# RWKV-7 recurrence of a two-layer decoder step: when the rows of v, the keys and the bonus product are issued

## The chip, the cores and the metric

The kernel runs on one core of a Trainium2 chip. The metric is the device time of one execution in microseconds; the time shown for a kernel is the median of its runs.

## What is computed

One inference step of two layers over a prompt of 2048 tokens (16 meta tokens ahead of it) and a sample batch of 8 x 4 tokens, width 1024. Layer 0 is sliding-window attention, layer 1 is RWKV-7 time mixing with 16 heads of 64. The change lies in the second one:

```python
def step(S, inp):                      # per token, S is (value, key) per head
    r_t, w_t, k_t, v_t, a_t, b_t = inp
    sa = jnp.einsum('bhvk,bhk->bhv', S, a_t)
    S = S * w_t + sa[..., None] * b_t + v_t[..., None] * k_t
    return S, jnp.einsum('bhvk,bhk->bhv', S, r_t)

y = (y - mean) * lax.rsqrt(var + GN_EPS)       # per head
y = y * ln_g + ln_b
bonus = jnp.sum(r_h * k_h * r_k, axis=-1, keepdims=True) * v_h
y = (y + bonus) * jax.nn.silu(g)
out = jnp.einsum('btw,wd->btd', y, w_out)
```

The final hidden state is normalised and returned, with the new attention window, the state S and the shift row.

## The kernel before, in words

The first two thirds of the program compute attention and the projections of the second layer, and leave their results in DRAM: keys and decay factors (bk), receptance and the like (ar), v, a bonus factor per token and head (bo), gates and first-layer outputs. The last third, from about 1580 us on, is the recurrence. It goes over 17 units of the prompt: a unit of meta tokens, then 16 units of 128 tokens, each of four chunks of 32 tokens. The tokens of a chunk are done at once; the state S goes from chunk to chunk.

*A chunk* is `chain` (line 1422). PE multiplies the state block Z with L into C (C<-Z,L), ACT copies the result to R0s, PE multiplies with TT, the inverse of a triangular matrix per head (C<-R0s,TT), ACT writes that into Z, PE multiplies Z with the transposed keys LS (C<-Z,LS), and DVE scales the result by the decay pe into the Z of the next chunk (Z<-C,pe). There are four Z in turn; their rows of v come by DMA (Z<-v).

*Ahead of time*, for later units: `keys` (1374) transposes BK on PE into kt and ACT copies it to LS; `scores` (948) multiplies L with BK into pz, which ACT copies to LAs and DVE masks back into L; `inverse` (976) sends LAs through DRAM (la_d) to LA, one row per chunk and head, and POOL solves the triangular systems in some sixty small products (XT<-LA,X and X<-X,XT), scales them (X<-X,ln) and sends them through DRAM (tt_d) to TT. The unit two further on (s in the code) gets its scores while unit u runs, and the inversion for the next unit runs on POOL at that time.

*Behind the chain*: `outputs` (1465) gives Y for two chunks at a time. `group_norm` (1583) of a unit runs during the next one, in steps between yields: it fetches the rows of v again (vt), takes the mean, multiplies vt by the bonus (line 1602), subtracts the mean into ytm, and lets ACT square it; DVE sums the squares into var, POOL takes the root (lines 1621 and 1622), and DVE scales ytm by var, lng and lnb and adds vt. `gate` and `project_out` multiply by the gate, transpose, and project with `dense_steps`.

*The order of the work* is written by hand. `steady` (1765), for units 2 to 14, runs per chunk: first product, left-over steps of the last chunk, side work (Y, scores, key transposes of the next unit in chunk 3), a step of the norm, the solve, keys of the unit's own second half in chunk 0, another step of the norm, the state update, loads. `in_order` (1752) then binds DVE, ACT and POOL to the order in which this was written. DMAs of SP are not bound by it: they are placed by a scheduler, behind the last Z load that was written ahead of them (`released`, 1405). A queue works in order: a DMA at its head that waits holds those behind it. Without an engine named, a load goes out on SP; with `s_` on ACT.

In `steady`, BK and the second half of L of the unit two on are loaded on ACT after the chunk's third step in chunk 0 (lines 1832 to 1837), and half 0 of L for the unit three on in chunk 3 (1841), so that it is there when its unit comes to be the second one on. There are four BK tiles, two to a unit, so BK of unit s takes the place of unit u's, once its keys are transposed; six L tiles; two vt tiles; one h tile and one ytm tile.

Of the kernel before, what the change touches and what calls it, by code (L numbers as in the profile page):

```python
# [14 lines left out]
ALU = mybir.AluOpType  # L15
# [15 lines left out]
def tile_hybrid_step(ctx: ExitStack, tc: tile.TileContext, a, o, c):  # L31
# [842 lines left out]
    def all_of(gen):  # L874
        for _ in gen:
            pass
# [391 lines left out]
    with ExitStack() as ph:  # L1268
# [314 lines left out]
        def group_norm(u):  # L1583
# [12 lines left out]
            for x in range(2):  # L1596
                ms_ = mean[:n, x * 8:x * 8 + 8]
                v_.tensor_reduce(out=ms_, in_=u.Y[x][:n], axis=AX.X, op=ALU.add)
                v_.tensor_scalar(out=ms_, in0=ms_, scalar1=1.0 / 64, scalar2=None, op0=ALU.mult)
                if vts and x == 0:  # L1600
                    for e in range(2):
                        tt(v_, vts[e], vts[e], u.bont[:n, 8 - e * 8:16 - e * 8].unsqueeze(2).broadcast_to([n, 8, 64]), ALU.mult)
                    yield MARK
                if x == 0:
                    u.ytm = u.Ys if u.kind == "s" else lt.tile([P, 2, 8, 64], F32, name="ytm", tag="ytm", bufs=1)
                    y = u.ytm[:n].rearrange("p e g d -> p (e g) d")
                for e, ps_ in HS:
                    if u.kind == "s" and e == 0:
                        tt(v_, u.ytm[:n, x], u.Y[x][:n], ms_.unsqueeze(2).broadcast_to([n, 8, 64]), ALU.subtract)
                    elif u.kind != "s":  # L1610
                        tt(v_, u.ytm[64 * x:64 * x + 64, e], u.Y[x][ps_],
                           mean[ps_, x * 8:x * 8 + 8].unsqueeze(2).broadcast_to([64, 8, 64]), ALU.subtract)
                yield MARK if vts and x == 0 else 2.3
# [6 lines left out]
            with tc.high_priority(offset=5000):  # L1620
                g_.tensor_scalar(out=var[:n], in0=var[:n], scalar1=1.0 / 64, scalar2=64e-5, op0=ALU.mult, op1=ALU.add)
                tt(g_, var[:n], var[:n], mhalf[:n], ALU.pow)
            yield MARK
            tt(v_, y, y, bc(var), ALU.mult)
            yield MARK
# [139 lines left out]
        def steady(i, u, pe):  # L1765
# [9 lines left out]
            for ch in range(4):  # L1775
# [36 lines left out]
                run(pe[ch], 1.2)  # L1812
                next(rec)
                with released():
                    if ch == 0 and i > 2:
                        all_of(keys(u, 1))
                    if ch == 3:
                        all_of(kt)
                        inv[s.idx] = inverse(s)
                        next(inv[s.idx])  # L1820
                    else:
                        next(inv.get(i + 1, idle()), None)
                if ch < 3:
                    run(norm, to=MARK)
                else:
                    norms_[u.idx] = group_norm(u)
                    run(norms_[u.idx], to=MARK)
                    run(norms_[u.idx], to=MARK)
                run(pe[ch], 1.9)
                next(rec, None)  # L1830
                with released():
                    if ch == 0:
                        first = L0s.pop(s.idx, None)
                        load_BK(s, s_)
                        s.L.append(first or load_L(s, 0, s_))
                        s.L.append(load_L(s, 1, s_))
                        small_loads(s)
                    if ch == 2 and i + 1 in inv:
                        load_TT(us[i + 1])
                    if ch == 3 and i + 3 < len(us):  # L1840
                        L0s[i + 3] = load_L(us[i + 3], 0, s_)
                run(pe[ch], to=MARK)
                rests.append(pe[ch])
                for part in PLAN.get((i, ch), ()):
                    with released():
# [214 lines left out]
```

## Time and profile before

| | |
|---|---|
| median of 3 runs | 2597.73 us (2594.54 to 2601.28) |
| profiled execution | 2601.98 us, span of its instructions 2600.2 us |
| busy share of the span | PE 86%, PEld (weight loads) 60%, DVE 65%, ACT 45%, POOL 40% |
| mean granted clock of TensorE | 0.937 of full speed |
| moved by DMA | 312.99 MB, 120 GB/s over the span |
| chain that ended last, by engine | PE 50%, DVE 18%, issue 10%, ACT 9%, DMA 8%, POOL 4% |

The shares are averages over stages that differ. The recurrence's steady part, some 1720 to 2420 us, is the stage that the change touches; there a row of the timeline tells when an instruction started, how long it took, how long its engine had been idle before it and what ended that. "issue" as a releaser means that the profile shows nothing that was waited for. SPq and ACTq rows are DMA issues on those queues, not transfers.

### The profile page before, as it was taken

Reading aid. Unit: us, or ns where it says so; the run is one execution under the profiler, and the core shown is the slowest. Engines: PE = TensorE matmul, PEld = TensorE weight load, DVE = VectorE, ACT = ScalarE, POOL = GpSimd, SP = SyncE. Lnnn points to the kernel's source line nnn. Section 1 sums busy time; section 2 is a strip of 40 time slices with the busy share of each in tenths; the row PEclk is TensorE's granted clock in tenths of the full one; section 3 lists DMA queues with packets and bytes.
Section 4 is the critical chain, followed back from the end, with each engine's and each line's share of the span. In section 5 each row is a group of like instructions: output and inputs, shape, how many; then the busy total and the mean of one; then the engine's idle time right before and its main releaser. Section 6 shows DMA issues by size and latency. Waiting matters only on the chain.

```text
span 2600.2 us, 60852 instructions
## 1 busy us (share of the span) xinstructions
PE 2238.5 (86%) x24932; PEld 1547.7 (60%) x24932; DVE 1687.0 (65%) x3181; ACT 1169.5 (45%) x2799; POOL 1044.8 (40%) x1572
## 2 busy tenths in 40 slices
PE   6999999899999898999999997567777777777897
PEld 5877777767845446676666785354444444444553
DVE  7586675567749887665656665645666566666684
ACT  6676455555523335454434444233443434434432
POOL 4242123222112335433333333147566666656613
PEclk9999999999999998999999998778898988889999
DMA  8433122331447664322222216564544545454423
GB/s 202 122 106 117 63 69 94 107 115 62 150 138 226 210 205 153 98 81 96 86 102 85 93 67 192 140 182 118 132 105 114 135 115 131 103 126 124 106 67 76
DMA packets 346235, 312.99 MB, mean 120 GB/s; under 512 B 205546, under 2 KB 282218, under 8 KB 344131
## 3 DMA queue, kind: packets, MB, share of 16 engines
q1 hardware_dynamic: 327219, 278.03, 36.4%
q10 hardware_dynamic: 17120, 27.27, 4.0%
q0 software_dynamic: 1616, 3.79, 0.7%
q8 instruction: 196, 3.21, 0.5%
q14 instruction: 84, 0.69, 0.1%
HBM read 191.15 MB, written 119.84 MB: 120 GB/s over the span
## 4 chain that ended last, share of the span: by engine, by line
PE 50%; DVE 18%; issue 10%; ACT 9%; DMA 8%; POOL 4%; SPq 2%; POOLq 0%; ACTq 0%; DVEq 0%
PE pd L38 29%; PE po L38 5%; PE C L38 5%; DVE xm L47 4%; DMA BK<-bk 2%; DVE xpr L44 2%; ACT ssb L41 2%; PE pz L38 2%; SPq L50 2%; PE Y L38 2%; PE sc L38 1%; PE oT L38 1%; DMA wst<-in_rwkv_w_in 1%; DMA L<-ar 1%; PE kt L1385 1%
## 5 line engine op out<-in xcount | busy, mean ns | idle before, releaser
L38 PEld LDWEIGHTS <-yp 128*128 128x128 f16 x1488 | 141.1, 99 | 165.2 <-issue 12.8
L47 DVE SCALAR_TENSOR_TENSOR xm<-dx,mu,xn 128x256 f32<-128x256 f32 (+2 forms) x432 | 199.8, 523 | 48.9 <-POOL dx L44 47.6
L44 POOL TENSOR_TENSOR X<-X,XT 128x126 f32<-128x126 f32 (+24 forms) x458 | 202.4, 442 | 35.5
L44 POOL TENSOR_TENSOR XT<-LA,X 128x126 f32<-128x126 f32 (+24 forms) x458 | 180.4, 394 | 39.7 <-DVE X L44 6.0
L38 PE MATMUL C<-Z,L 128*32 128x64 f32 x2048 | 49.5, 247 | 170.4 <-issue 159.9
L38 PE MATMUL pd<-xp,wq 128*128 128x256 f16 (+2 forms) x1728 | 186.0, 266 | 11.4 <-DVE qp L47 8.0
L38 PE MATMUL pd<-wg,xg 128*128 128x512 f16 (+1 forms) x816 | 193.1, 384 | 0.7 <-issue 0.7
L38 PE MATMUL po<-wo,yp 128*128 128x512 f16 x768 | 188.9, 389 | 0.0
L38 PE MATMUL pd<-wvv,xpr 128*128 128x512 f16 (+1 forms) x816 | 187.4, 387 | 0.0
L38 PE MATMUL pd<-xpr,w 128*128 128x256 f16 (+2 forms) x1728 | 186.0, 267 | 0.0
L38 PE MATMUL pd<-xp,wg 128*128 128x256 f16 (+2 forms) x1728 | 182.6, 266 | 0.9 <-DVE xp L44 0.5
L38 PE MATMUL pd<-xpr,wkk 128*128 128x256 f16 (+2 forms) x1728 | 179.5, 264 | 0.0
L38 PEld LDWEIGHTS <-wq 128*128 128x128 f16 x1728 | 159.3, 99 | 32.7 <-DVE qp L47 9.2
L44 POOL TENSOR_TENSOR ssb<-ssb,bias 128x512 f32<-128x512 f32 x64 | 86.4, 1355 | 223.9 <-DVE ssb L462 185.5
L38 PEld LDWEIGHTS <-w 128*128 128x128 f16 x1728 | 157.5, 99 | 27.0 <-issue 9.7
L38 PEld LDWEIGHTS <-wg 128*128 128x128 f16 x1728 | 159.2, 99 | 21.5 <-issue 4.0
L38 PEld LDWEIGHTS <-wkk 128*128 128x128 f16 x1728 | 158.2, 98 | 15.6 <-issue 0.4
L38 PE MATMUL pd<-w,yp 128*128 128x512 f16 x720 | 162.9, 384 | 3.3 <-DMA yp<-y 3.3
L44 POOL TENSOR_TENSOR ps<-wst,ps 128x1024 f16<-128x1024 f32 x32 | 69.5, 2171 | 220.0 <-ACT wst L41 201.7
L38 PEld LDWEIGHTS C<-Z,L 128*32 128x32 f32 x2048 | 38.9, 126 | 195.8 <-issue 192.3
L41 ACT ACTIVATE R0s<-C 128x256 f32<-128x256 f32 x65 | 25.0, 385 | 274.9 <-PE C L38 269.9
L38 PEld LDWEIGHTS <-xpr 128*128 128x128 f16 (+1 forms) x816 | 79.1, 100 | 102.6 <-issue 17.5
(357 smaller groups left out, 4913.2 us busy)
## 6 DMA issues: line engine op xcount, KB each, us to landing
wst<-in_rwkv_w_in SPq DMA_DIRECT2D x32, 512.0 KB
wsp<-ps SPq DMA_DIRECT2D x32, 512.0 KB
x<-in_x_prompt SPq DMA_DIRECT2D x29, 512.0 KB
xn<-xn SPq DMA_DIRECT2D x14, 1028.0 KB
ar<-aro SPq DMA_DIRECT2D x28, 512.0 KB
bk<-bko SPq DMA_DIRECT2D x28, 512.0 KB
BK<-bk ACTq DMA_DIRECT2D x26, 512.0 KB
L<-ar ACTq DMA_DIRECT2D x52, 256.0 KB
```

The costliest lines, as they stand in the source:

```text
L38: return t_.matmul(out=out, lhsT=lhsT, rhs=rhs, start=start, stop=stop, **kw).ins
L41: return s_.activation(out=out, in_=in_, func=func, **kw).ins
L44: return e.tensor_tensor(out=out, in0=in0, in1=in1, op=op).ins
L47: v_.scalar_tensor_tensor(out=out, in0=in0, scalar=scalar, in1=in1, op0=op0, op1=op1)
L50: return (eng or nc.sync).dma_start(out=out, in_=in_).ins
L1385: t_.transpose(out=ps[:w * 64, j].rearrange("p e d -> p (e d)"), in_=u.BK[half][:, j, 2 * c2:2 * c2 + w, :].rearrange("p c x -> p (c x)"), ...
```

## The change

It does four things in the recurrence. In `group_norm` the multiplication of vt by the bonus moves from ahead of the subtraction of the mean to behind the variance, into a step of its own, and `steady` runs one step of the norm more at the end of chunk 0. The norm of a unit is begun, and so its vt requested, at the end of chunk 2 instead of in chunk 3. BK and the first half of L for the unit two on are requested on SP, right behind the key transposes of chunk 0 and ahead of the copies to LS; only the second half of L stays on ACT. And the loading of L for the unit three on now stands under `if ch == 3` inside `if ch == 2`, so it is never reached, and every first half of L is loaded in chunk 0's code.

```diff
--- before.py
+++ after.py
@@ -1598,8 +1598,6 @@
                 v_.tensor_reduce(out=ms_, in_=u.Y[x][:n], axis=AX.X, op=ALU.add)
                 v_.tensor_scalar(out=ms_, in0=ms_, scalar1=1.0 / 64, scalar2=None, op0=ALU.mult)
                 if vts and x == 0:
-                    for e in range(2):
-                        tt(v_, vts[e], vts[e], u.bont[:n, 8 - e * 8:16 - e * 8].unsqueeze(2).broadcast_to([n, 8, 64]), ALU.mult)
                     yield MARK
                 if x == 0:
                     u.ytm = u.Ys if u.kind == "s" else lt.tile([P, 2, 8, 64], F32, name="ytm", tag="ytm", bufs=1)
@@ -1620,6 +1618,9 @@
             with tc.high_priority(offset=5000):
                 g_.tensor_scalar(out=var[:n], in0=var[:n], scalar1=1.0 / 64, scalar2=64e-5, op0=ALU.mult, op1=ALU.add)
                 tt(g_, var[:n], var[:n], mhalf[:n], ALU.pow)
+            yield MARK
+            for e, vt in enumerate(vts):
+                tt(v_, vt, vt, u.bont[:n, 8 - e * 8:16 - e * 8].unsqueeze(2).broadcast_to([n, 8, 64]), ALU.mult)
             yield MARK
             tt(v_, y, y, bc(var), ALU.mult)
             yield MARK
@@ -1812,8 +1813,13 @@
                 run(pe[ch], 1.2)
                 next(rec)
                 with released():
-                    if ch == 0 and i > 2:
-                        all_of(keys(u, 1))
+                    if ch == 0:
+                        kt = keys(u, 1) if i > 2 else idle()
+                        next(kt, None)
+                        first = L0s.pop(s.idx, None)
+                        load_BK(s)
+                        s.L.append(first or load_L(s, 0))
+                        all_of(kt)
                     if ch == 3:
                         all_of(kt)
                         inv[s.idx] = inverse(s)
@@ -1823,23 +1829,23 @@
                 if ch < 3:
                     run(norm, to=MARK)
                 else:
-                    norms_[u.idx] = group_norm(u)
-                    run(norms_[u.idx], to=MARK)
                     run(norms_[u.idx], to=MARK)
                 run(pe[ch], 1.9)
                 next(rec, None)
                 with released():
                     if ch == 0:
-                        first = L0s.pop(s.idx, None)
-                        load_BK(s, s_)
-                        s.L.append(first or load_L(s, 0, s_))
                         s.L.append(load_L(s, 1, s_))
                         small_loads(s)
                     if ch == 2 and i + 1 in inv:
                         load_TT(us[i + 1])
+                if ch == 2:
+                    norms_[u.idx] = group_norm(u)
+                    run(norms_[u.idx], to=MARK)
                     if ch == 3 and i + 3 < len(us):
                         L0s[i + 3] = load_L(us[i + 3], 0, s_)
                 run(pe[ch], to=MARK)
+                if ch == 0:
+                    run(norm, to=MARK)
                 rests.append(pe[ch])
                 for part in PLAN.get((i, ch), ()):
                     with released():
```

DVE at the boundary between two units and in the first chunk of the next, before (vt are rows of v, Z_19045 the state that chunk 0 begins with; Y has a number per unit):

```order
L47 SCALAR_TENSOR_TENSOR yp<-yps,yp 128x512
L1598 TENSOR_REDUCE mean<-Y_22365 128x8
L1599 TENSOR_SCALAR mean<-mean 128x8
L44 TENSOR_TENSOR vt<-vt,bont 128x512 x2
L44 TENSOR_TENSOR Z_19045<-C,pe 64x256 x4
L47 SCALAR_TENSOR_TENSOR gt<-gt,pd 128x512
```

and now:

```order
L47 SCALAR_TENSOR_TENSOR yp<-yps,yp 128x512
L1598 TENSOR_REDUCE mean<-Y_22365 128x8
L1599 TENSOR_SCALAR mean<-mean 128x8
L44 TENSOR_TENSOR Z_19045<-C,pe 64x256 x4
L47 SCALAR_TENSOR_TENSOR gt<-gt,pd 128x512
L44 TENSOR_TENSOR gt<-gt,ytm 128x512
```

The multiplication has left the place ahead of Z_19045. It stands now a chunk later, behind Z_19046, the state for chunk 1:

```order
L1616 TENSOR_REDUCE var<-Y_22714 128x8
L44 TENSOR_TENSOR Z_19046<-C,pe 64x256 x4
L47 SCALAR_TENSOR_TENSOR h_22753<-po,h_22753 128x512
L44 TENSOR_TENSOR vt<-vt,bont 128x512 x2
L44 TENSOR_TENSOR ytm<-ytm,var 128x1024
L44 TENSOR_TENSOR L<-pz,smk 64x512 x4
```

SP at the end of a unit, before (la_d, LA, tt_d and TT belong to the inversions, pe and bont are the decay and bonus factors):

```order
L50 DMA la_d<-LAs 32x32x32 x2
L50 DMA pe<-pe_169 128x32
L50 DMA bont<-bo_205 128x16
L50 DMA tt_d<-X 64x16x32 x2
L50 DMA LA<-la_d 64x1024 x2
L50 DMA vt<-v_104 128x512
L50 DMA TT<-tt_d 64x1x512 x2
L50 DMA vt<-v_104 128x512
L50 DMA out_y_prompt<-h_21362 128x1024
L50 DMA h_22060<-h_3_86 128x1024
```

and now:

```order
L50 DMA la_d<-LAs 32x32x32 x2
L50 DMA L<-ar_156 64x1024
L50 DMA tt_d<-X 64x16x32 x2
L50 DMA LA<-la_d 64x1024
L50 DMA vt<-v_104 128x512 x2
L50 DMA LA<-la_d 64x1024
L50 DMA TT<-tt_d 64x1x512 x2
L50 DMA L<-ar_156 64x1024
L50 DMA pe<-pe_169 128x32
L50 DMA bont<-bo_205 128x16
L50 DMA out_y_prompt<-h_21357 128x1024
L50 DMA h_22055<-h_3_86 128x1024
```

Both vt stand between the two LA and ahead of both TT; half of L stands ahead of tt_d and half behind TT; pe and bont have gone behind them.

ACT in chunk 0, behind the squares (Y), before:

```order
L41 ACTIVATE Y_21667<-ytm 128x512
L41 ACTIVATE Y_22021<-ytm 128x512
L50 DMA BK<-bk_147 128x4x256 x2
L50 DMA L<-ar_156 64x1024 x2
L41 ACTIVATE R0s<-C 128x256
L41 ACTIVATE po,ssq_22061<-h_22060 128x512
```

and now:

```order
L41 ACTIVATE Y_21667<-ytm 128x512
L41 ACTIVATE Y_22016<-ytm 128x512
L50 DMA L<-ar_156 64x1024 x2
L41 ACTIVATE R0s<-C 128x256
L41 ACTIVATE po,ssq_22056<-h_22055 128x512
L41 ACTIVATE LAs<-pz 32x2x128 x4
```

The two BK requests are gone from ACT. SP in the same chunk 0 now, from the rows of v for chunks 2 and 3 on:

```order
L50 DMA Z_19044<-v_105 32x512
L50 DMA Z_19047<-v_105 32x512 x2
L50 DMA Z_19044<-v_105 32x512
L50 DMA xg<-xg_128 128x16x128
L50 DMA BK<-bk_147 128x4x256 x2
L50 DMA Z_19046<-v_106 32x512
```

BK has left ACT and stands on SP behind xg, the gate's input; the pair of L requests that ACT made in chunk 3 for the unit three on is gone, and the first half of L is the one that SP has taken over above.

## Rows read from the trace of the kernel before

**Rows 1.** Waits, all engines, 1850 to 2340 us: engine line waited for: us in total, times, longest
```profile
DVE vt L44 <- DMA vt<-v: 90.4, 18, 7.7
POOL LA L44 <- DMA LA<-la_d: 72.8, 10, 7.6
POOL var L1621 <- DVE var L1618: 62.1, 9, 7.7
```

**Rows 2.** Timeline of DVE: start us, us, engine line op tiles, count [idle before <-releaser]
```profile
2180.55 2.07 DVE L44 TENSOR_TENSOR vt<-vt,bont 128x512 f32<-128x512 f32 x1 [1.95 <-DMA vt<-v]
2189.11 0.97 DVE L44 TENSOR_TENSOR vt<-vt,bont 128x512 f32<-128x512 f32 x1 [6.49 <-DMA vt<-v]
2190.00 1.72 DVE L44 TENSOR_TENSOR Z<-C,pe 64x256 f32<-64x256 f32 x4
```

**Rows 3.** Timeline of PE, chunk 0 of a steady unit
```profile
2191.82 1.08 PE L38 MATMUL C<-Z,L 128*32 128x64 f32 x32 [9.02 <-issue]
...
2194.54 1.08 PE L38 MATMUL C<-R0s,TT 32*32 32x64 f32 x32
...
2197.34 1.04 PE L1385 MATMUL kt<-ident,BK 128*128 128x128 f32 x8
```

**Rows 4.** Timeline of SP, which issues DMAs, at the same boundary
```profile
2174.17 1.28 SPq L50 DMA_DIRECT2D LA<-la_d  x2
2175.50 0.58 SPq L50 DMA_DIRECT2D vt<-v  x1
2176.17 1.10 SPq L50 DMA_DIRECT2D TT<-tt_d  x2
2177.37 0.38 SPq L50 DMA_DIRECT2D vt<-v  x1
```

**Rows 5.** Windows: stretch, us, busy PE PEld DVE ACT POOL, PEclk, DMA share, GB/s
```profile
2186.00:2188.00 2.00, 0.00 (x0) 0.00 (x0) 0.00 (x0) 0.00 (x0) 1.62 (x5) 0.50 0.13 50
```

**Rows 6.** Timeline of POOL over one period
```profile
2171.11 1.58 POOL L44 TENSOR_TENSOR X<-X,ln 128x512 f32<-128x512 f32 x1
2180.15 1.92 POOL L44 TENSOR_TENSOR LA<-LA,ln 128x1024 f32<-128x1024 f32 x1 [7.46 <-DMA LA<-la_d]
...
2196.69 0.46 POOL L44 TENSOR_TENSOR X<-X,XT 128x128 f32<-128x128 f32 x1
2203.48 0.20 POOL L1621 TENSOR_SCALAR var<-var 128x16 f32<-128x16 f32 x1 [6.33 <-DVE var L1618]
...
2207.15 1.33 POOL L44 TENSOR_TENSOR X<-X,XT 128x135 f32<-128x135 f32 x1
...
2224.18 1.28 POOL L44 TENSOR_TENSOR X<-X,ln 128x512 f32<-128x512 f32 x1
```

**Rows 7.** Timeline of POOL, ends of the first and the last of twelve inversions
```profile
1797.35 1.26 POOL L44 TENSOR_TENSOR X<-X,ln 128x512 f32<-128x512 f32 x1
...
2385.06 1.64 POOL L44 TENSOR_TENSOR X<-X,ln 128x512 f32<-128x512 f32 x1
```

**Rows 8.** Timelines of SP, DVE and PE at the last boundary of the part
```profile
2391.04 1.06 SPq L50 DMA_DIRECT2D vt<-v  x2
...
2392.71 1.09 SPq L50 DMA_DIRECT2D TT<-tt_d  x2
...
2397.02 1.41 DVE L44 TENSOR_TENSOR vt<-vt,bont 128x512 f32<-128x512 f32 x2 [2.90 <-DMA vt<-v]
...
2402.67 0.52 PE L38 MATMUL C<-R0s,TT 32*32 32x64 f32 x18
```

**Rows 9.** Chain that ended last, in order of time: start us, us, what
```profile
2200.83 6.66 DMA BK<-bk
...
2234.35 10.71 issue
```

**Rows 10.** Timelines of PE, SP and POOL in the first steady unit
```profile
1729.00 3.32 PE L38 MATMUL pz<-L,BK 64*64 64x64 f32 x64 [7.26 <-DMA L<-ar]
...
1754.11 1.09 SPq L50 DMA_DIRECT2D LA<-la_d  x2
...
1760.00 2.28 POOL L44 TENSOR_TENSOR LA<-LA,ln 128x1024 f32<-128x1024 f32 x1 [33.61 <-DMA LA<-la_d]
```

## The prediction

> **What bounds the kernel now.** I read the list of waits first, then the timelines of DVE, PE, SP and POOL over one period of the recurrence, then the chain that ended last. In nine periods of the steady part DVE waited 90.4 us for rows of v in the multiplication by the bonus, and POOL waited 72.8 us for LA and 62.1 us for the variance [rows 1]. The timeline of DVE shows what the first of these does: the first multiplication waits until 2180.55, the second until 2189.11, and only behind them stands the state update Z, 2190.00 to 2191.72 [rows 2]. PE starts the next unit's C at 2191.82, after 9.02 us of nothing, and its product with TT (I call it the solve) at 2194.54 [rows 3]. So rows that are needed late in a unit hold up the state that is needed first.
>
> Why are the second rows late? SP issued both requests within 1.9 us, one ahead of the two TT requests and one behind them [rows 4]; the first was there about 5 us after its issue, the second 11.7 us. In the last part of that time the DMA engines were 0.13 busy, about two of sixteen, and the clock of TensorE had gone to 0.50, its level of 1.2 GHz [rows 5]: a tail on two engines, with PE idle. I infer that it is TT's tail, since it is what stands between the two requests.
>
> POOL has its own loop. It ends one inversion at P = 2172.69 (2171.11 + 1.58), SP then writes out X (tt_d) and fetches LA, and POOL starts the next inversion at 2180.15. It comes to the variance at 2197.15, waits 6.33 us there, goes on at 2203.48 and ends at 2225.46 [rows 6]. Work is 17.0 + 22.0 = 39.0 us, the waits some 7.3 (LA) and 6.9 (variance) on average [rows 1]. Eleven periods lie between P = 1798.61 and P = 2386.70, 53.46 us each [rows 7].
>
> **The change, part by part.** *The multiplication moves.* Two instructions of DVE, 1.41 us together when nothing disturbs them [rows 8], leave the place ahead of Z and come back behind the next chunk's Z and the first sum into h. The wait for the rows, 90.4 / 9 = 10.0 us a period, leaves the state's path; the rows are then needed behind Z of the next chunk, P + 16.0 + 8.9 + 1.7 by the numbers below, about P + 26.6, and came at P + 16.4 (2189.11). What is late next? Two things, and the later one sets the new period.
>
> First POOL. Nothing shortens its 39.0 us. The requests for vt now stand between the two for LA on SP, so the second LA is issued two requests later, 1.2 us at the 0.58 of [rows 4], and the data of vt, 512 KB, go ahead of it. At the start of the steady part both vt already stand ahead of LA, and LA came 4.8 us after the last issue (1755.20 to 1760.00) [rows 10], against 4.7 in the period shown (1.28 behind 2174.17, so 2175.45, to 2180.15) [rows 4, 6]: so bounds of 0 and 2 us for the data, and I take 0.5, near the row. The multiplications now fall into the stretch after the variance. A product of POOL that ran beside the scaling of ytm on DVE took 1.33 us where its neighbour took 0.46 [rows 6], 0.9 lost beside an operation of 1.4; I take 0.9 for the two multiplications, with 0 and their whole 1.4 as bounds. The Trainium skill (SBUF — State Buffer, Who interferes with whom) says that VectorE and GpSimd share a port pair as an exclusive lock, held for a whole instruction. By that rule both multiplications would cost POOL their full 1.4 us, and the sum below would be 5 us smaller in its gain; the row agrees in kind. The variance is ready 8.9 us after the solve (2194.54 to 2203.48) [rows 3, 6]. POOL would come to it at P + 9.0 + 17.0 = P + 26.0 and the solve (next paragraph) is at P + 16.0, so the variance is ready at P + 24.9: the wait of 6.9 is gone. POOL's new period: 7.3 + 1.2 + 0.5 + 39.0 + 0.9 = 48.9 us.
>
> Second TT. It is now issued behind both vt. The last boundary of the part shows that order already: vt twice at 2391.04, TT twice at 2392.71, the solve at 2402.67, which is P + 16.0 with P = 2386.70 [rows 7, 8], while at the period shown the solve came at P + 21.9. Period by this loop: 16.0 to the solve, 8.9 to the variance, 22.0 + 0.9 to the next P, 47.8 us. POOL's 48.9 is the longer, by 1.1.
>
> The chain on PE is shorter than both: from a solve at 2194.54 it has work up to 2234.35, where the next idle stretch begins [rows 9], 39.8 us; with 2.7 from C to solve [rows 3] some 42.5, so 6.4 us to spare.
>
> So a period goes from 53.46 to 48.9, and **11 periods save 11 x 4.56 = 50 us**.
>
> *Key loads behind the transposes, on SP.* Two BK requests leave ACT for SP, where they stand behind h, four Z and xg. Now they are issued at 2200.4 and the last lands at 2207.49 [rows 9], 12.9 us after the solve. The transposes end at 2198.38 [rows 3], so they can come at best 2 us sooner, and later by as much as SP is held at h, whose request waits for the output rows to leave the same tile. I take 0: up to 6.4 us to either side stay inside what the chain has to spare. That is the cover; without it each us of a late BK is a us of the period. Behind BK on SP stand only the rows of v for the next unit, which wait for PE in the second half of the unit anyway. The half of L that SP now takes from ACT goes out ahead of tt_d while SP would wait for POOL, and the other half behind TT: 1.1 us of issue, nothing on POOL's loop.
>
> *The first steady unit.* There PE waited 7.26 us for L at 1729.00, and POOL had been idle for 33.6 us when LA came at 1760.00 [rows 10], so an earlier score is an earlier inversion. L and BK are now requested before or between the weights, some 5 us and more sooner. I take 5 us: 7.3 less the 1.2 for two L requests ahead of la_d and about 1 for queueing. Bounds 0 and 8.
>
> **Sum.** 50 + 5 = 55 us. The profiled execution took 2601.98 us (span 2600.2), 4.25 above the median of 2597.73. 2601.98 - 55 = 2547; against the median 2597.7 - 55 = **2543 us**.
>
> **The rivals.** *More than that.* If neither LA nor TT comes later than at their best rows, POOL does 39.0 + 7.3 and TT's loop 16.0 + 8.9 + 22.0 = 46.9: a gain of 6.6 x 11 + 8 = 80 us, 2518. For it: the last boundary [rows 8]. Against it: LA is issued behind vt in every steady period. It would go lower still if the new order of the queue shortened TT's own tail. The Trainium skill (DMA: Bandwidth & Descriptors, Why a DMA increments its semaphore by 16 and not by 1) says that a copy goes to as many engines as divide its slowest dimension on both sides; TT's source has two there, so two engines, in any order. The 0.13 of [rows 5] agrees. Chance 0.10.
>
> *Less.* The half megabyte of vt and a quarter of L ahead of LA and TT cost 3 us instead of 0.5, or tt_d lands later behind L. Period 51.5, 11 x 2.0 + 3 = 25 us, 2573. For it: the two engines that carry TT are the ones with a tail, and all of that data passes them too. Chance 0.20.
>
> *Nothing.* The wait for vt is replaced in full by one for TT and LA, because every queue that moves up pushes them back, 4.5 us in each period, and only the start gives a little: 2595. Chance 0.07.
>
> *Slower.* Key loads on SP. Place: BK behind h and xg. PE's scores wait for BK, and the scores feed LAs, la_d and so the next LA. The chain has 6.4 us to spare, and 4.56 more until the old period: it decides if BK lands more than 11 us later after the solve than now, at 24 instead of 12.9. At 27 the period is 56.6, 3.1 x 11 = 35 us slower, 2632. For it: SP works in order, and h ahead of BK waits for the output rows. Against it: BK's last half took 6.7 us once issued [rows 9], so its issue would have to slip by all of the 11. Chance 0.06.
>
> **How the numbers follow.** Forecast 0.57 (2530 to 2557: period 48 to 50, start 3 to 8), more 0.10, less 0.20, nothing 0.07, slower 0.06. The range 2520 to 2578 holds the forecast, the rival of less and the upper half of more, about 0.82. A measurement of this kernel can tell 0.3%, 7.8 us. Faster by over 0.3%: 0.57 + 0.10 + 0.20 = 0.87; within: 0.07; slower: 0.06.
>
> **What would show it.** In the list of waits DVE's wait for vt is gone from the steady part, and POOL's for the variance falls from 6.9 to under 1.5 us a period. POOL's wait for LA grows from 7.3 to about 9. The period between two X<-X,ln is 48 to 50 us, and PE's idle stretch moves from ahead of C to ahead of the solve, about 5 us long. The two multiplications stand behind Z of chunk 1, 0.7 us each. If POOL still waits 5 us and more for the variance, TT is later than P + 16 and the step on TT is wrong; if PE's wait for BK grows past 3 us a period, the step on the key loads is. If the period is above 52, the forecast is wrong as a whole.

## The result, and the profile after

The changed kernel takes 2565.75 us (median of 4 runs, 2560.01 to 2572.44) against 2596.14 for the kernel before beside it (2592.95 to 2601.28): ratio 0.988, 95% interval 0.985 to 0.991. It is faster, by 30 us, where 55 were forecast. The profiled execution took 2572.44 us, its span is 2570.7, 29.5 less than the 2600.2 before.

Lines from the list of waits over the same stretch, 1850 to 2340 us (engine, line, waited for: us in total, times, longest), which answer to [rows 1]:

```profile
POOL LA L44 <- DMA LA<-la_d: 65.6, 6, 11.6
PE pz L38 <- DMA BK<-bk: 41.9, 15, 4.6
POOL LA L44 <- DMA pe<-pe: 32.0, 3, 11.4
PE C L38 <- DMA TT<-tt_d: 17.6, 12, 2.2
POOL LA L44 <- DMA bont<-bo: 9.3, 1, 9.3
POOL ms L1704 <- ACT po L41: 7.1, 4, 3.5
```

DVE's wait for vt and POOL's for the variance are gone from the list. The three lines of POOL for LA are one wait (what ended it is inferred by the profile, and the three names differ): 106.9 us in ten periods, 10.7 each where it was 7.3. Two waits have come up: PE's for BK, 4.2 us a unit, and POOL's for ms, the scale that POOL makes from the sum of squares of the output rows. POOL's timeline, with the first and the last of the twelve inversions and one period between, answers to [rows 6, 7]:

```profile
1803.98 1.26 POOL L44 TENSOR_TENSOR X<-X,ln 128x512 f32<-128x512 f32 x1
...
2151.06 1.67 POOL L44 TENSOR_TENSOR X<-X,ln 128x512 f32<-128x512 f32 x1
2164.09 1.92 POOL L44 TENSOR_TENSOR LA<-LA,ln 128x1024 f32<-128x1024 f32 x1 [11.36 <-DMA pe<-pe]
2181.26 0.20 POOL L1619 TENSOR_SCALAR var<-var 128x16 f32<-128x16 f32 x1
2197.24 0.19 POOL L1704 TENSOR_SCALAR ms<-ssq 128x2 f32<-128x2 f32 x1 [1.62 <-ACT po L41]
...
2352.08 1.27 POOL L44 TENSOR_TENSOR X<-X,ln 128x512 f32<-128x512 f32 x1
```

With P at the end of X<-X,ln, P goes from 1805.24 to 2353.35 in eleven periods: **49.83 us each**, 53.46 before. SP's timeline at that boundary answers to [rows 4]: one request for LA has come to stand behind both vt.

```profile
2153.39 1.34 SPq L50 DMA_DIRECT2D tt_d<-X  x2
2154.83 1.31 SPq L50 DMA_DIRECT2D LA<-la_d  x1
2156.24 1.01 SPq L50 DMA_DIRECT2D vt<-v  x2
2157.30 0.48 SPq L50 DMA_DIRECT2D LA<-la_d  x1
2157.98 1.11 SPq L50 DMA_DIRECT2D TT<-tt_d  x2
...
2173.26 3.52 SPq L50 DMA_DIRECT2D BK<-bk  x2
```

PE, one unit earlier, starts the solve at 2115.72, waits for the second part of TT, and later waits twice for BK [rows 3, 9]:

```profile
2115.72 0.30 PE L38 MATMUL C<-R0s,TT 32*32 32x64 f32 x4 [0.58 <-DMA TT<-tt_d]
2118.27 0.64 PE L38 MATMUL C<-R0s,TT 32*32 32x64 f32 x28 [2.25 <-DMA TT<-tt_d]
...
2131.16 0.81 PE L38 MATMUL pz<-L,BK 64*64 64x64 f32 x32 [0.78 <-DMA BK<-bk]
2134.39 1.13 PE L38 MATMUL pz<-L,BK 64*64 64x64 f32 x32 [2.42 <-DMA BK<-bk]
```

The 29.5 us by stage. PE's first key transposes lie at 1605.01 in the kernel before and at 1610.37 here. Up to there PE has the same instructions in the same order, so these 5.4 us are two executions differing; over all kernels of this study that row starts between 1598.0 and 1613.6. From it to the first P: 193.6 before, 194.9 here. Eleven periods: -40.0. From the last P to the end: 213.5 before, 217.3 here. Sum: 5.4 + 1.3 - 40.0 + 3.8 = -29.5.

### The profile page after: what moved, and what is told of

Same layout as the page of the kernel before. It is cut to its first block, busy times and chain, and to the rows that moved or that the text cites. A ratio compares the mean times of both kernels' runs of the same rounds, so it can differ in the third digit from the quotient of the medians.

```text
span 2570.7 us, 60893 instructions
## 1 busy us (share of the span) xinstructions
PE 2257.2 (88%) x24932; PEld 1549.3 (60%) x24932; DVE 1680.7 (65%) x3181; ACT 1168.5 (45%) x2799; POOL 1040.5 (40%) x1572
## 4 chain that ended last, share of the span: by engine, by line
PE 38%; DVE 19%; DMA 15%; POOL 9%; ACT 8%; issue 7%; SPq 4%; POOLq 0%; ACTq 0%; DVEq 0%
PE pd L38 22%; PE po L38 5%; DVE xm L47 4%; SPq L50 4%; DMA BK<-bk 4%; DMA TT<-tt_d 3%; PE C L38 3%; DVE xpr L44 2%; POOL X L44 2%; DMA wst<-in_rwkv_w_in 2%; PE pz L38 2%; ACT ssb L41 2%; POOL XT L44 2%; PE sc L38 1%; DMA L<-ar 1%
## 5 line engine op out<-in xcount | busy, mean ns | idle before, releaser
L44 POOL TENSOR_TENSOR X<-X,XT 128x126 f32<-128x126 f32 (+24 forms) x458 | 195.7, 427 | 35.7
L38 PE MATMUL po<-wo,yp 128*128 128x512 f16 x768 | 203.9, 412 | 0.0
L38 PE MATMUL pd<-xp,wg 128*128 128x256 f16 (+2 forms) x1728 | 188.8, 271 | 0.9 <-DVE xp L44 0.5
L44 DVE TENSOR_TENSOR Z<-C,pe 64x256 f32<-64x256 f32 x256 | 108.0, 422 | 67.8 <-PE C L38 46.3
L38 PEld LDWEIGHTS <-xpr 128*128 128x128 f16 (+1 forms) x816 | 79.0, 100 | 102.4 <-issue 17.2
L44 DVE TENSOR_TENSOR xpr<-xm,xpr 128x512 f16<-128x512 f32 (+2 forms) x144 | 98.8, 707 | 56.8 <-ACT xpr L41 56.4
L41 ACT ACTIVATE ssb<-ssb,ng 128x128 f32<-128x128 f32 (+1 forms) x272 | 104.2, 384 | 59.7 <-DVE es L44 55.9
```

The lines of the kernel that those rows point to most:

```text
L38: return t_.matmul(out=out, lhsT=lhsT, rhs=rhs, start=start, stop=stop, **kw).ins
L41: return s_.activation(out=out, in_=in_, func=func, **kw).ins
L44: return e.tensor_tensor(out=out, in0=in0, in1=in1, op=op).ins
```

## The experiments

All were timed in 3 rounds beside the kernel before. The columns below are means over the eleven periods of each profiled execution, relative to P (landings are from the trace's DMA events): the period; when POOL starts on LA; when PE starts the solve; when the last of BK lands; and what POOL waited besides, for the variance and for ms. What is left of a period is POOL's work. The edits are shown in short; `...` marks lines left out.

```
run                     ratio [95%]            period  LA    solve  BK    var+ms  work
kernel before           1                      53.46   7.2   22.0   35.0  7.4     38.9
changed kernel          0.988 [0.985, 0.991]   49.83  10.7   13.0   31.5  0.9     38.2
m1_multiply_alone       0.980 [0.976, 0.983]   48.56   7.2   12.4   30.0  3.4     37.9
m2_keys_alone           0.981 [0.978, 0.983]   47.99   7.2   14.2   30.5  3.1     37.6
m3_keys_undone          1.014 [1.011, 1.017]   56.04  17.2   11.6   30.4  0       38.9
m4_rows_sooner_alone    1.008 [1.006, 1.010]   54.93  16.7   11.5   30.6  0       38.2
c1_rows_as_before       0.983 [0.980, 0.985]   48.36   7.5   13.0   30.7  3.6     37.3
d1_second_L_later       0.981 [0.979, 0.983]   47.90   9.2   12.0   27.6  0.1     38.6
c3_both                 0.979 [0.976, 0.981]   46.83   7.0   11.5   26.9  0.9     38.9
c4_both_TT_in_four      0.972 [0.970, 0.975]   46.39   6.9    9.9   24.4  0       39.5
d4_TT_in_four           0.979 [0.977, 0.980]   48.46   9.1   10.2   27.7  0       39.4
e3_LA_on_ACT            1.021 [1.019, 1.024]   57.81  18.8   15.0   26.5  0       39.0
e4_LA_ahead_of_tt_d     0.953 [0.950, 0.956]   42.61   3.8    9.7   21.6  0       38.8
f1_LA_first_alone       0.988 [0.983, 0.992]   50.16   7.5   14.5   30.7  4.3     38.3
```

**One part at a time.** The multiplication alone:

```diff
-                    for e in range(2):
-                        tt(v_, vts[e], vts[e], ..., ALU.mult)
...
+            yield MARK
+            for e, vt in enumerate(vts):
+                tt(v_, vt, vt, ..., ALU.mult)
...
+                if ch == 0:
+                    run(norm, to=MARK)
```

> Of the three parts of the change only one: the multiplication of the rows of v by the bonus stands behind the variance; rows of v and key loads are requested where the kernel before requests them. On SP both requests for LA then stand right behind tt_d again, the first vt behind them. P is the end of an inversion on POOL. Theory A (POOL's loop sets the period, and LA comes to it at P + 10.6 in the changed kernel because one LA request and its data stand behind 512 KB of vt): LA is back at about P + 7.3, POOL's work is 39.0 + 0.9, period 47.2 instead of the 49.8 measured in the changed kernel, 11 x 2.6 = 29 us less than 2565.8, about 2537 (2528 to 2547). Rival B (the key loads BK, late on SP, hold the scores and with them LA, whatever SP's order of vt and LA): the key loads are early here too, so B also expects about 2537, but lays it to BK; the kernel with the key loads alone undone tells the two apart. Rival C (the multiplication gives nothing by itself; the wait moves to TT): period 52 to 53, 2580 to 2596.

Measured: 0.980, LA back at P + 7.2. The period is 48.56 instead of 47.2: A's order is right, but POOL now waits 3.4 us for the variance and ms, so another loop has come close. By B's words this run alone doesn't tell the two apart. Lines from the waits of this kernel, 1850 to 2340 us:

```profile
PE C L38 <- DMA TT<-tt_d: 28.1, 13, 4.5
PE pz L38 <- DMA BK<-bk: 24.1, 12, 4.9
POOL ms L1704 <- ACT po L41: 23.3, 6, 5.3
POOL var L1619 <- DVE var L1616: 10.6, 6, 2.3
```

The key loads alone:

```diff
+                        load_BK(s)
+                        s.L.append(first or load_L(s, 0))
...
-                        load_BK(s, s_)
-                        s.L.append(first or load_L(s, 0, s_))
...
-                    if ch == 3 and i + 3 < len(us):
-                        L0s[i + 3] = load_L(us[i + 3], 0, s_)
```

> Only the key loads are moved: BK behind the key transposes on SP, the first half of L on SP too; rows of v are requested in the old place of the program and multiplied ahead of the state. In SP's queue both vt now stand ahead of TT and behind both LA. Theory A (key loads have no part in it): vt lands some 10 us after P, Z and C follow, solve at about P + 16, variance 8.9 later, P' 22.0 after it: period 46.9 to 49, the gain comes from vt standing ahead of TT's slow transfer, and the time is about 2535 to 2555. Rival B (BK on SP arrives some 6 us later behind the solve than on ACT and the scores wait for it): the period cannot fall under the 49.8 of the changed kernel: 2560 to 2570. The prediction's slower rival: over 2600.

Measured: 0.981. The move of key loads changes where the scheduler puts the other requests: vt, vt, TT, TT behind both LA, so vt is in time although it is still multiplied ahead of the state (DVE's wait for it is 8.5 us in all). Either of these two parts alone gives more than the whole change. Its period of 47.99 lies inside A's range and below the 49.8 that B gave as a floor; but PE's wait for BK and POOL's for ms are the next things in its list:

```profile
PE pz L38 <- DMA BK<-bk: 40.1, 13, 4.9
POOL ms L1703 <- ACT po L41: 31.8, 10, 6.3
```

The changed kernel with the key loads as before:

```diff
-                        load_BK(s)
-                        s.L.append(first or load_L(s, 0))
...
+                        load_BK(s, s_)
+                        s.L.append(first or load_L(s, 0, s_))
...
+                    if ch == 3 and i + 3 < len(us):
+                        L0s[i + 3] = load_L(us[i + 3], 0, s_)
```

> The changed kernel with the key loads as before (BK and L on ACT); rows of v requested a chunk sooner and multiplied behind the variance as in the changed kernel. SP's order comes out as tt_d, vt, vt, LA, TT, TT, LA. Theory A: the second LA now stands behind both vt and both TT, about 1.1 us of issue later than in the changed kernel, so LA comes at P + 11.5 to 12.5 and the period is 50.5 to 52: 2573 to 2590, slower than the changed kernel although BK is early. Rival B (BK late on SP holds the period): BK is early here, so the period falls by the 4.5 us that PE waits for BK in a unit or a good part of it: 2515 to 2545.

And the rows of v sooner alone:

```diff
-                    norms_[u.idx] = group_norm(u)
-                    run(norms_[u.idx], to=MARK)
...
+                if ch == 2:
+                    norms_[u.idx] = group_norm(u)
+                    run(norms_[u.idx], to=MARK)
```

> Only the rows of v are requested a chunk sooner; they are still multiplied ahead of the state, and the key loads are as before. SP's order is tt_d, vt, vt, LA, TT, TT, LA. Theory A: vt lands at about P + 8, so the state waits little for it; LA comes at P + 11.5 to 12.5 as in the run with the key loads undone, and POOL needs 39.0 behind it: period 50.5 to 52, 2570 to 2590. Theory B: BK is early, so the period is that of the solve at P + 15 to 16 + 8.9 + 22.0 = 46 to 47: 2520 to 2535. If the wait for vt is what counts by itself and only its request matters, half of it at least goes: under 2560.

Measured: 1.014 and 1.008, both slower than the kernel before, in A's direction and far beyond its size. SP and POOL of the run with the key loads undone:

```profile
2194.53 2.04 SPq L50 DMA_DIRECT2D vt<-v  x2
2196.66 0.49 SPq L50 DMA_DIRECT2D LA<-la_d  x1
2198.07 1.10 SPq L50 DMA_DIRECT2D TT<-tt_d  x2
2199.22 0.50 SPq L50 DMA_DIRECT2D LA<-la_d  x1
```
```profile
2210.43 1.91 POOL L44 TENSOR_TENSOR LA<-LA,ln 128x1024 f32<-128x1024 f32 x1 [17.37 <-DMA LA<-la_d]
```

The second LA stands behind TT and lands 11.2 us after its issue (means: P + 5.85 to P + 17.03), where it took 4.3 ahead of TT in the kernel before (P + 2.73 to 7.08). So the second LA comes in with TT, and POOL with it. B had forecast its best times for these two runs, and is out as the only cause; A had the order and the direction, but put LA 1 to 2 us later than in the changed kernel, and it came 6 later. So the part "rows requested sooner" by itself costs, and the part "key loads" is worth 2.6% here, by what it does to SP's order.

**Two edits, apart and together.** Undo the earlier request for vt, and ask for the second half of L, which goes out on ACT beside BK, a chunk later:

```diff
+                    norms_[u.idx] = group_norm(u)
+                    run(norms_[u.idx], to=MARK)
                     run(norms_[u.idx], to=MARK)
...
-                if ch == 2:
-                    norms_[u.idx] = group_norm(u)
-                    run(norms_[u.idx], to=MARK)
```
```diff
-                    if ch == 0:
-                        s.L.append(load_L(s, 1, s_))
+                    if ch == 1:
+                        s.L.append(load_L(s, 1, s_))
```

> The changed kernel with one part undone: rows of v are requested a chunk later, in the place of the kernel before (the multiplication stays behind the variance, the key loads stay on SP). The order of SP's queue differs from the changed kernel's in one place: LA, LA, vt, vt in place of LA, vt, vt, LA. Theory A (the changed kernel's period of 49.8 us is POOL's: LA at P + 10.6, then 39.2 us): LA comes back to P + 7.2, POOL alone could do 46.4, and the next bound is PE's chain with its wait for BK, 48.0 in the run with the key loads alone; so 47.5 to 48.5, 11 x 1.8 = 20 us under the changed kernel, ratio to the kernel before 0.978 to 0.983. Rival B (the changed kernel's period is already that of PE's chain with BK late): nothing changes, ratio 0.986 to 0.990.

> The changed kernel, with the second half of L (two loads on ACT) requested a chunk later, so that nothing on ACT is requested beside BK, which should then land 2 to 3 us sooner; SP's order is the changed kernel's. Theory A: LA stays at P + 10.6 and the period at 49.8; PE's wait for BK falls from 3.8 us a unit to 1 to 2 and nothing comes of it: ratio 0.986 to 0.990. Rival B: the period falls by what BK gains, 2 to 3 us, 22 to 33 us in all: ratio 0.975 to 0.980.

> Both of the two edits: rows of v requested as in the kernel before, and the second half of L a chunk later. Under theory A with PE's chain as the next bound both limits fall: POOL's 46.4 and a chain of 48.0 less the 2 to 3 us of BK; period 46.4 to 47, 11 x 1.0 to 1.6 = 11 to 18 us under the run with the rows as before, ratio 0.971 to 0.977. If the chain is held by something other than BK there, the ratio stays at 0.978 to 0.983.

Measured: 0.983, 0.981, 0.979. The first came out as A said, the second not: A expected nothing of an earlier BK, and the period fell by 1.9 us; B expected all of what BK gains, which is 3.9, and 0.981 lies outside its range too. The third came out between its two: the period of 46.83 lies in the 46.4 to 47 expected, the ratio is that of the case in which nothing is gained. Lines from the waits of the run with the second half of L later:

```profile
POOL LA L44 <- DMA LA<-la_d: 63.5, 7, 9.6
PE C L38 <- DMA TT<-tt_d: 54.9, 22, 3.6
...
PE pz L38 <- DMA BK<-bk: 0.3, 1, 0.3
```

BK lands at P + 27.6 instead of 31.5, PE's wait for it is gone, the scores are ready sooner, and la_d lands 1.8 us before P instead of 1.1 behind it. With la_d and half of L out of the way, SP starts tt_d at P, the second LA is issued at P + 3.8 instead of 4.2 and lands 5.3 us later instead of 6.4: LA at P + 9.2. (In the changed kernel fifteen of the sixteen rises of LA's semaphore have come after 5.2 us, and the last alone makes it 6.4; what holds that one is not shown.) So the LA that POOL waits for is late for two reasons, SP's order and late scores; I call this theory AB. Undoing the order alone leaves the late BK (PE's wait 42.5 us, POOL's for ms 37.3 in that run's list); undoing both gives a period of 46.8.

**TT in four requests,** on the kernel with both edits and on the changed kernel:

```diff
-            for gh in range(2):
-                dma(u.TT[64 * gh:64 * gh + 64]..., u.tt_d[:, gh:4:2].rearrange("k q x -> q k x"))
+            for q in (0, 2, 1, 3):
+                r0 = 64 * (q % 2) + 32 * (q // 2)
+                dma(u.TT[r0:r0 + 32]..., u.tt_d[:, q])
```

> As the run with both edits, and TT is fetched by four requests, one for each quarter q of tt_d, each with 32 rows in its slowest dimension, in place of two with 2 there. If a TT request is carried by two DMA engines only, as inferred from the 0.13 of all sixteen in the kernel before, its last part should land at about P + 11 instead of P + 14 and the solve follow it; two more issues of about 0.55 us each stand behind LA, so LA doesn't move. The solve starts PE's chain: if the chain still sets the period, up to 2 us a unit, ratio 0.968 to 0.973; if POOL's own 46.4 does by then, nothing: same as the run with both edits within 0.2%. If TT's landing stays at P + 14, the inference on two engines is wrong.

> The changed kernel, with TT fetched by four requests (one for each quarter q of tt_d) in place of two; rows of v, key loads and both halves of L as in the changed kernel. Theory AB, formed from the runs so far (POOL's loop and PE's chain are coupled: LA comes late both because one of its requests stands behind vt and because la_d, which needs the scores, which need BK, is late): TT lands at about P + 10.5 instead of P + 14.8, the solve and with it the key transposes and the request for BK move up by 3 us, la_d lands before the inversion ends, LA comes at P + 9.2 as in the run with the second half of L later, POOL does 38.7 behind it: period 47.9, ratio 0.978 to 0.984. Theory A alone (only SP's order of vt and LA counts): period 49.8, ratio 0.986 to 0.990.

Measured: 0.972 with the two edits, 0.979 in the changed kernel alone. TT lands at P + 10.0 instead of 14.2, and at 10.2 instead of 14.8. In the changed kernel the DMA engines are 0.15 busy while PE waits for the rest of TT, with the clock at 1.00 (window 2116 to 2118 us), and in the four-request version 1.07 (2136 to 2138; a packet's whole time counts where it starts, so a share can pass 1):

```profile
2116.00:2118.00 2.00, 0.02 (x1) 0.00 (x0) 1.75 (x3) 0.00 (x0) 1.61 (x6) 1.00 0.15 56
```
```profile
2136.00:2138.00 2.00, 1.29 (x76) 0.99 (x68) 1.86 (x3) 0.42 (x2) 1.16 (x1) 1.00 1.07 233
```

So the tail is TT's own, as [rows 5] suggested, and no matter of PE's idle clock. In the changed kernel AB holds: LA at P + 9.1, period 48.46, a little above the 47.9 expected (POOL's work is 39.4 there). Its list of waits corrects one thing:

```profile
PE pz L38 <- DMA BK<-bk: 48.0, 14, 6.0
```

PE waits longer for BK here than in the changed kernel (48.0 us, 41.9 there), and LA comes 1.6 us sooner all the same. BK lands at P + 27.7, since the solve ahead of it is earlier, and la_d 1.3 us before P. So it is not the length of PE's wait for BK that counts, but when the scores are ready; a shorter TT mends that as well as an earlier BK does.

With both edits in, LA and POOL's work are nearly all of the period already, and it moves by 0.4 us only; the rest of that gain lies in the first steady units, 185.0 us from the first key transposes to the first P instead of 192.1, and in executions differing.

**LA earlier.** Two tries, on the kernel with both edits and TT in four. First la_d and LA on ACT's queue:

```diff
-                u.LAs[32 * e:32 * e + 32].rearrange(...))
+                u.LAs[32 * e:32 * e + 32].rearrange(...), s_)
...
+        if late:
+            yield
...
-            dma(LA[hh * 64:hh * 64 + nl], la_d.rearrange(...))
+            dma(LA[hh * 64:hh * 64 + nl], la_d.rearrange(...), s_)
...
+                    if ch == 3:
+                        next(inv[s.idx])
```

> The kernel with rows as before, the second half of L later and TT in four, and besides la_d and LA of the steady part on ACT's queue, right behind the scores' copies and ahead of the tanh of the next gate, so that LA no longer stands behind tt_d, which waits for the end of the inversion. There la_d landed 2.9 us before P and LA was issued at P + 1.9 and 2.7. Theory: LA is issued about a microsecond before P and lands some 3 us sooner, at P + 3 to 4; POOL's loop falls from 46.7 to 43 to 44; PE's chain (42.5 us of work and some 2 of BK) then sets the period, 44.5 to 45.5, ratio 0.961 to 0.968. Rival: ACT, which has to wait about 2.5 us for la_d ahead of LA, holds the tanh and the copy R0s of the state's path behind it: period 46.5 to 48, ratio 0.970 to 0.980.

Measured: 1.021, a miss by both theories. ACT's queue at one boundary:

```profile
2147.05 1.55 ACT L41 ACTIVATE LS<-kt 64x256 f32<-64x256 f32 x4
2148.47 0.34 ACTq L50 DMA_DIRECT2D la_d<-LAs  x1
...
2154.98 1.10 ACTq L50 DMA_DIRECT2D LA<-la_d  x2
2156.18 0.60 ACT L41 ACTIVATE gt<-pd 128x512 f32<-128x512 f32 x1 [6.03 <-issue]
```

la_d does not stand behind the copies of the scores, as I had read from the program, but behind the copies of the next unit's keys, at P + 6.7; and LA holds the tanh of the gate for 6 us while it waits for la_d. The rival had named this hold, at a smaller price.

Second, LA stays on SP, and tt_d is made to follow it:

```diff
+        if late:
+            yield
         for hh in range(2):
-            dma(tt_d[hh:32:2]..., X[hh * 64:hh * 64 + nl])
+            x = dma(tt_d[hh:32:2]..., X[hh * 64:hh * 64 + nl])
+            if late:
+                tc.add_manual_dep(x, LA_last[0].name, ...)
...
                         next(inv[s.idx])
+                        if i + 1 in inv:
+                            next(inv[i + 1], None)
+                            load_TT(us[i + 1])
...
-                    if ch == 2 and i + 1 in inv:
-                        load_TT(us[i + 1])
```

> The kernel with rows as before, the second half of L later and TT in four, and besides both requests for LA stand ahead of tt_d in SP's own queue (la_d stays where it was on SP), so that they no longer wait for the end of the inversion P. In the kernel it is built on, la_d landed at P - 2.9 and LA was issued at P + 1.9 and 2.7 and landed at P + 6.8. Theory (POOL's loop set its 46.7, by LA's place): LA is issued at about P - 2.5 and lands about P + 1.5 to 2.5; POOL's loop alone could do 42, so PE's chain, 42.5 us of work and 2 for BK, sets the period: 44 to 45.5, 11 x 1.2 to 2.7 = 13 to 30 us under the kernel it is built on, ratio to the kernel before 0.961 to 0.968. Rival (PE's chain already sets the 46.7): LA comes sooner and POOL waits for the variance instead, ratio 0.970 to 0.975.

Measured: **0.953** [0.950, 0.956], 2472.99 us: the fastest version, about 90 us under the changed kernel by the ratios. SP and POOL at one boundary:

```profile
2083.35 1.08 SPq L50 DMA_DIRECT2D LA<-la_d  x2
2084.84 1.33 SPq L50 DMA_DIRECT2D tt_d<-X  x2
2086.22 3.11 SPq L50 DMA_DIRECT2D vt<-v  x2
```
```profile
2083.54 1.28 POOL L44 TENSOR_TENSOR X<-X,ln 128x512 f32<-128x512 f32 x1
2089.28 1.91 POOL L44 TENSOR_TENSOR LA<-LA,ln 128x1024 f32<-128x1024 f32 x1 [4.46 <-DMA LA<-la_d]
...
2127.56 1.28 POOL L44 TENSOR_TENSOR X<-X,ln 128x512 f32<-128x512 f32 x1
```

The period of 42.61 is LA at P + 3.8 and POOL's 38.8. It is 3.8 us shorter where 1.2 to 2.7 were expected: PE's chain, put at 42.5 and 2 for BK, keeps up with 42.6 in all. LA was to land at P + 1.5 to 2.5 and lands at P + 3.6: it is issued at P - 1.5, just after la_d has landed (P - 1.6, as in the kernel it is built on, and not the P - 2.9 that the expectation took).

The same edit in the changed kernel, without the other edits:

> The changed kernel with one edit: tt_d is requested behind both LA (and, as SP's order then comes out, behind both vt): LA, vt, vt, LA, tt_d, tt_d, TT, TT. Rows of v, key loads, the second half of L beside BK and TT in two requests stay as in the changed kernel. In the changed kernel la_d lands at P + 1.2. Theory A alone (LA's wait behind tt_d and vt is the whole of it): LA lands at P + 5 to 7 and the period falls to 44 to 46, ratio 0.965 to 0.975. Theory AB (PE's chain, with BK late and TT's slow tail, holds la_d): la_d is what LA then waits for, tt_d stands behind it on SP and is held as well, and the chain's 48 us, seen with the rows as before, remain: period 47.5 to 49.5, ratio 0.978 to 0.988.

Measured: 0.988, the changed kernel's own ratio. LA comes at P + 7.5, and POOL waits for the variance instead, since tt_d and TT are what is late now: TT lands at P + 17.2. AB's ratio is just met, but its period is not (50.16, 47.5 to 49.5 expected), and the wait is not the one AB named. Lines from the waits, and SP:

```profile
PE C L38 <- DMA TT<-tt_d: 62.1, 20, 4.9
POOL var L1626 <- DVE var L1623: 36.4, 10, 4.2
```
```profile
2150.78 1.35 SPq L50 DMA_DIRECT2D tt_d<-X  x2
2152.18 4.15 SPq L50 DMA_DIRECT2D bont<-bo  x1
2158.10 1.10 SPq L50 DMA_DIRECT2D TT<-tt_d  x2
```

## Why the prediction was right, and where it was wrong

The sign, the range (2520 to 2578) and the mechanism held: the wait for vt leaves the state's path, and the period is POOL's, LA's arrival plus its work. But the gain of 55 us was put 25 too large, and the time lies nearer to the rival of less (2573) than to the forecast. By stage, the eleven periods gave 40 of the 50 us forecast, the first steady units lost 1.3 where 5 were to be gained, the end lost 3.8 that were not in the sum, and 5.4 were lost ahead of the first key transposes, where the two executions differ. That the period came so near, 49.8 for 48.9, is in part luck: two terms were too small by 2.6 us together, and a third was too large by 1.7. Step by step:

- *The multiplication moves.* Right. It stands behind Z of the next chunk, 1.52 us for both (2178.86 us on DVE), and nothing waits for the rows. Moved alone, it gives a ratio of 0.980.
- *POOL's new period, 48.9.* Measured 49.83. LA was put at 9.0 (7.3 + 1.2 + 0.5) and comes at 10.65; the work at 39.9 and is 38.2; and 0.9 for ms was not in the sum. The work is shorter because POOL's sixty products took 25.65 us a period in place of 26.50; that they vary (24.6 to 27.1 us over these kernels) was not in the sum either. The LA term was mis-sized, 3.4 us over before instead of 1.7: the second LA is issued 1.5 later (1.2 forecast) and takes 2.0 longer to land (0.5 forecast, at the upper of the two bounds). With BK early and SP's order the same, LA came at 9.2, so the order costs 2.0 of the 3.4, near the forecast, and late scores 1.4.
- *TT comes later, solve at P + 16.0.* Earlier in fact, P + 13.0 for the first part and 2.5 more for the second. PE is held 0.6 and 2.3 us there, not in one stretch of 5. The variance was in time, as forecast.
- *Key loads behind the transposes: "I take 0".* **This step failed.** BK's last half landed 12.9 us behind the solve before; now it is issued at P + 22.1 and lands at P + 31.5, 18.5 behind the first part of the solve. That is 5.6 later, inside the 6.4 us that I had PE's chain to spare. But the spare was counted for this wait alone: the same chain now also waits for TT's second part (1.8 us a unit), and BK's 4.2 us come on top. Chain and waits still fit in the period (42.5 + 1.8 + 4.2 = 48.5 of 49.8, an estimate from these rows); what they delay is the scores, la_d with them, and so LA. The run with the second half of L later takes this cost away: 1.9 us a period (1.4 at LA, 0.8 at ms, less 0.3 of work), 11 x 1.9 = 21 us, and by the ratios 0.007 of 2596 or 19 us. That is more than the 10 us by which the periods missed their forecast, because the work put too long hid the rest. TT in four takes nearly as much away, 1.4 us a period, and leaves PE's wait for BK: late BK and TT's tail stand one behind the other in one chain, and it is enough to mend either. So the sign that the text named, a wait for BK above 3 us a unit, did appear, but does not by itself tell the cost. It is not SP as such that makes BK late: with rows as before and the multiplication moved, the period is 48.56 with key loads on ACT and 48.36 on SP. What delays BK there is the half of L beside it (landing 9.2 us after the issue with it, 6.0 without).
- *The first steady unit, 5 us.* 1.3 us were lost instead. From the first key transposes to the first P the runs took 189 to 196 us, whether key loads were moved or not, and 183 to 185 in all four with TT in four requests: so a shorter TT is worth 7 us and more there, and an earlier L nothing that shows.
- *The end* was not in the sum. All six kernels with the key loads moved and TT in two requests take 215.9 to 218.0 us from the last P on, the four with the key loads as before 211.6 to 213.5. With TT in four it is 212.2 to 215.1. Some 4 us; why, no run here settles.
- *Rivals.* "Slower" named the right place, BK, with a threshold too far out: it needs no 11 us, since it acts through la_d and LA before the chain itself sets the period. The rival of a lower TT tail was right in kind: by the rule of the Trainium skill (DMA: Bandwidth & Descriptors, Why a DMA increments its semaphore by 16 and not by 1) two rows in the slowest dimension mean two engines, and with 32 there TT came 4 to 5 us sooner. And a wait that takes the place of the one removed is what the two runs with rows sooner and key loads as before show in full.
- *POOL beside the multiplications, 0.9.* Somewhat too large. In the period shown, the product of 128x136 elements beside them took 0.88 us instead of 0.42 a period earlier, its neighbour 0.74 instead of 0.41, 0.8 lost beside 1.5. In eight of the eleven units 0.7 to 0.8 us were lost so; in the other three no product ran beside them. By the port rule as the prediction read it (SBUF — State Buffer, Who interferes with whom, in the Trainium skill) it would have been the whole 1.5.

```profile
2178.94 0.88 POOL L44 TENSOR_TENSOR X<-X,XT 128x136 f32<-128x136 f32 x1
2179.91 0.74 POOL L44 TENSOR_TENSOR XT<-LA,X 128x128 f32<-128x128 f32 x1
```
```profile
2128.78 0.42 POOL L44 TENSOR_TENSOR X<-X,XT 128x136 f32<-128x136 f32 x1
2129.28 0.41 POOL L44 TENSOR_TENSOR XT<-LA,X 128x128 f32<-128x128 f32 x1
```

## What to carry to other kernels

Where several loops pass through one queue, count the slack of a loop once for all waits that the change puts into it, and not afresh for each. Read an edit's effect in the order that the queue ends up with: here a request moved up cost more than the wait it removed (1.008), and requests moved to another engine's queue were worth 2.6% because others changed places with them. When the engine that bounds the loop is idle for a transfer whose data are already there, put that request ahead of whatever waits for the same engine: once BK and TT were no longer late, that was worth 2%; in the changed kernel, with both late, nothing (0.988).

## What the runs showed of the hardware

A transfer issued behind one that runs on few DMA engines gets that one's tail. The trace has the times at which a transfer's semaphore rises: sixteen times for LA, vt and BK, three times for TT, the first 1 us after its issue. For LA behind TT (key loads undone) fourteen rises have come 5.1 us after the issue and the last two after 10.8 and 11.2, means over eleven periods, and in each of the eleven the last two come only after some 10 us or more; ahead of TT, in the kernel before, all sixteen have come after 4.3. The second rows of v in the kernel before, whose wait began this study, show the same behind TT: fourteen after 4.9, the last two after 10.7 and 11.1. So the tail on two engines that [rows 5] let one infer is seen: two rises of sixteen wait for TT's last, and POOL or DVE waits for those two.

TT as two requests with 2 rows in the slowest dimension landed about 9 us after its last issue; as four with 32 rows its semaphore rises sixteen times, and it landed about 4 us after (P + 5.5 to 14.8, and P + 6.0 to 10.2), though SP issues two requests more.
